# Emitting the output projection's weights earlier, with more raw buffers, in a hybrid encoder layer

## The chip, the core and the metric

The kernel runs on one core of a Trainium2 chip. The metric is the device time of one execution in microseconds, as the median of the runs. The core has a matrix engine (TensorE, PE in the profile, with its weight loads shown apart as PEld), a vector engine (VectorE, DVE), a scalar engine (ScalarE, ACT), GpSimd (POOL) and a sync engine (SP) that here only issues transfers. Each engine works through its own queue in order; semaphores tie the queues together. ACT and POOL issue some transfers too.

## The reference, cut to what matters

One encoder layer on 1024 tokens of width 1024: a half-step feed-forward, a mixer with two groups of heads side by side, and a second half-step feed-forward. The change sits in the mixer's output projection.

```
h = pre2(x); z = h @ w_in
y_att  = attention_group(z[..., :1536])          # 512 columns, normalised per head, times attn_out_g
y_rwkv = rwkv7_group(z[..., 1536:])              # 512 columns: two scans summed, group norm, bonus, gate
mix = concatenate([y_att, y_rwkv], -1) @ w_out   # w_out: 1024 x 1024
h = h + rmsnorm(mix, mix_post_g)
f = swiglu(rmsnorm(h, ffn2_pre_g), w_gate, w_up, w_down)
h = h + 0.5 * rmsnorm(f, ffn2_post_g)
```

All of it is float32 in and out. The first 512 rows of `w_out` meet the attention half, the last 512 the scan's half.

## The kernel before

**Products.** Float32 operands are split in two parts of a reduced form, `h` (a copy rounded by ACT) and `l` (the rest, by DVE), and a product is three matrix products: `h*h`, `h*l`, `l*h`. `load` (L181) issues the transfer and `split` (L184) does the two steps; so each weight tile costs one transfer into a raw buffer, one ACT and one DVE instruction. For the attention half the split also multiplies by a gain (L1054, L1055).

**Order on the queues.** The program is written against a framework that takes the source's order as a rank, works out by itself in which order each engine's instructions are issued, places the semaphores, and lets the tiles of a pool wait for what lay in the same memory before. A pool's tag has a fixed number of buffers; a tile waits until the one that held its buffer is read for the last time. Pools are stacks on two sides of the on-chip memory.

**The stages round the change**, in `run` (L1163):

- Values, attention and the scan's inputs are made; a step `prep(n)` (L783) prepares block `n` of eight, `solve(n)` (L850) inverts its triangular systems on DVE in some 62 short instructions, `merge(n)` (L875) assembles the inverses, and `chain(n)` (L918) carries the scan's state through the block. `upto(m)` (L1283) runs `prep` and `solve` up to block `m`. Lines L800 and L810 to L832 are parts of `prep`, L866 to L870 of `solve`, L937 to L970 of `chain`.
- `out_weights` (L1041) loads and splits eight tiles of 128 x 512 (four row groups `k`, two column halves `dh`) with tag `wor` for the raw tile (one buffer), `woh` and `wol` for the parts (eight each). For the attention half it is called at L1294, behind `upto(2)`.
- `project_attended` (L1066) takes one tile of 128 tokens of the attention's result through its half of the projection: two groups of twelve matrix products into `po` (L1064), copied to `yao` (L1083; the same tag `wor`, so the same single buffer) and stored to `hp`. It runs once per block, two at the first, between the chains.
- `finish_half` (L1035) runs four units of the group norm (`finish_unit`, L975): six loads of 256 KB and one of 128 KB (`f_y`, `f_k`, `f_r`, `f_v`, `f_sg`), two sums on POOL (L994, L997), five small products on PE (L995 to L1025), and at the end the split (L1028) into the operand `x`. The pool `fin0` holds three units at a time. Units 0 and 1 fill the columns of row tiles 0 and 1, units 2 and 3 those of 2 and 3, and so on. The first half is called at L1310, the second at L1322; units of the second half need the last block's chain.
- `out_weights` for the scan's half is called between them, at L1320, with a pool `wo` of its own.
- `out_project` (L1086) takes the eight row tiles: load of the row from `hp` (L1090), 24 matrix products `pw` (L1064), sums on DVE (L1095), and then `done(i)`: `post` (L251 to L258: load of `res`, a sum of squares on ACT into `junk`, L256, L257, store), `pre` of the row before (L266), and the turning for the next feed-forward (L330). From the fifth row tile on, POOL forms sums and differences of rows (L339 to L343).

**Where the pools lie.** Bytes per partition in the program before:

```
left    scan 75,392-108,544   (its last tile, xs: 106,496-108,544)
        eo  108,544-150,016   (rs, wor/yao 1 x 2,048, woh, wol, yat, yah, yal)
   then rows2 75,264-108,032, wo 108,032-142,848 (wor 1 x 2,048, woh, wol),
        hand2 142,848-159,488 (b_mix_post_g, res, junk, rs1, b_ffn2_pre_g)
right   fin0 152,512-194,560 (g2w, three each of f_y0, f_y1, f_k0, f_k1, f_r, f_v, f_sg), closed before hand2 opens
```

Of the kernel before, what the change touches and what calls it, by code (L numbers as in the profile page):

```python
# [10 lines left out]
F32 = mybir.dt.float32  # L11
# [152 lines left out]
class _Kernel:  # L164
# [202 lines left out]
    def down(self, p, ring, rows, psum, hid, wd, ws, order, done):  # L367
# [11 lines left out]
        def right(n, m):  # L379
            if n > 3:  # L380
                src = ws[n - 4, m]
            else:
                r, c = {1: (0, 0), 2: (1, 0), 3: (1, 1)}[n]
                src = wd[(2 * m + r) * 128:(2 * m + r + 1) * 128, c * 512:(c + 1) * 512]
            return [q.rearrange("p a b -> p (a b)") for q in self.halves(
                p, self.slab(ring, src.rearrange("p (a b) -> p a b", a=4)), ("gh", "gl"), GB)]

        def left(n, m, cols):
            raw, h, l = (ring.tile([128, 512], dt, name="g" + t, tag=t, bufs=b)[:, :cols.stop - cols.start]
                         for t, dt, b in (("raw", F32, RAW), ("wh", F32R, WB), ("wl", F32R, WB)))  # L390
            self.load(raw, hid[n - 1, m, :, cols])
            self.split(h, l, raw)
            return h, l
# [9 lines left out]
        for q, n in enumerate((1, 2, 6, 5, 3, 7, 4)):  # L403
            W = {}
            for g in [(0, 1), (2, 3)] if n == 4 else [(0, 1, 2, 3)]:
                ps = [psum.tile([128, 512], F32, name="pd", tag=("d", "gu")[q % 2]) for i in g]
                for m in range(NM):
                    h, l = left(n, m, slice(g[0] * 128, g[-1] * 128 + 128))
                    if m not in W:
                        W[m] = right(n, m)  # L410
                    wh, wl = W[m]
                    for x in range(len(g)):
# [42 lines left out]
    def project_attention(self, p, psum, x, streams):  # L455
# [10 lines left out]
        zts = [p.tile([128, 4, 128], F32, name="zts", tag="zts", bufs=6) for t in range(6)]  # L466
        W = {0: q_w, 1: list(zip(kh, tiles(1, "l")))}
        for b in (1, 0):
            hl = self.columns(p, b * 512, 512, W[b], bufs=11)
            if b:  # L470
# [567 lines left out]
            for g in range(2):  # L1038
                self.finish_unit(p, psum, b, g, x, g2w)

    def out_weights(self, p, k0, gain=None):  # L1041

        nc, W = self.nc, []
        for k in range(4):
            hl = []
            for dh in range(2):
                raw = p.tile([128, 512], F32, name="wor", tag="wor", bufs=1)
                self.load(raw, self.io["w_out"][0][(k0 + k) * 128:(k0 + k + 1) * 128, dh * 512:(dh + 1) * 512])
                h = p.tile([128, 512], F32R, name="woh", tag="woh", bufs=8)
                l = p.tile([128, 512], F32R, name="wol", tag="wol", bufs=8)  # L1050
                if gain is None:
                    self.split(h, l, raw)
                else:
                    nc.scalar.activation(h, raw, AF.Copy, scale=gain[:, k:k + 1])  # L1054
                    nc.vector.scalar_tensor_tensor(l, raw, gain[:, k:k + 1], h, op0=OP.mult, op1=OP.subtract)  # L1055
                hl.append((h, l))
            W.append(hl)
        return W
# [7 lines left out]
    def project_attended(self, p, c, psum, t, W, rs_a):  # L1066

        nc, V, A, T = self.nc, self.nc.vector, self.nc.scalar, self.nc.tensor
        rows = slice(t * 128, (t + 1) * 128)
        y = p.tile([128, H, 64], F32, name="yat", tag="yat")  # L1070
        self.load(y.rearrange("p a b -> p (a b)"), self.ya_d[rows, :])
        V.tensor_tensor(y, y, rs_a[:, t * H:(t + 1) * H][:, :, None].to_broadcast([128, H, 64]), op=OP.mult)
        q = psum.tile([128, 4, 128], F32, name="yq", tag="eo")
        for k in range(4):
            T.transpose(q[:, k, :], y.rearrange("p a b -> p (a b)")[:, k * 128:(k + 1) * 128], self.ident)
        h, l = (p.tile([128, 4, 128], F32R, name="ya" + c, tag="ya" + c) for c in "hl")
        A.activation(h, q, AF.Copy)
        V.tensor_tensor(l, q, h, op=OP.subtract)
        for dh in range(2):
            ps = psum.tile([128, 512], F32, name="po", tag="eo")  # L1080
            self.out_products(ps, W, dh, h, l, slice(0, 128))
            o = p.tile([128, 512], F32, name="yao", tag="wor", bufs=1)
            A.copy(o, ps)  # L1083
            self.nc.scalar.dma_start(self.hp_d[rows, dh * 512:(dh + 1) * 512], o)

# [77 lines left out]
    def run(self):  # L1163
# [5 lines left out]
        with self.top as top:  # L1169
# [5 lines left out]
            x = self.operand(xp, xp)  # L1175
            x0 = self.io["x"][0]

            with ExitStack() as st:
# [11 lines left out]
                with self.tc.high_priority():  # L1190
                    gain = self.spread_row(hand, ring, pt, "ffn1_pre_g")
# [26 lines left out]
                p = self.pool(st, "ffn1")  # L1218
# [17 lines left out]
                x = x2  # L1236
# [40 lines left out]
            eo = self.pool(s_eo, "eo")  # L1277
# [5 lines left out]
            def upto(m):  # L1283
                while nxt[0] <= min(m, NB - 1):
                    n = nxt[0]
                    blk[n] = self.prep(n, sp, pp, R0 if n in (3, 5) else B0)
                    self.solve(n, sp)
                    nxt[0] += 1

            upto(1)  # L1290
            rs_a = self.rstd(eo, self.ss_a.rearrange("p a b -> p (a b)"), NT * H, 1.0 / HD, EPS)
            self.merge(0, blk[0], sc, pm)
            upto(2)
            WA = self.out_weights(eo, 0, self.aog)  # L1294
            for n in range(NB):
                if n:
                    self.merge(n, blk[n], sc, pm)
# [2 lines left out]
                for t in ([0, 1] if n == 0 else [n + 1] if n + 1 < NT else []):  # L1300
                    self.project_attended(eo, sc, pe, t, WA, rs_a)
            s_sr.close()
# [4 lines left out]
            x = self.operand(xr, xr, n=4)  # L1307
            fi = self.pool(s_fi, "fin0", 3, **R)
            pf = self.pool(s_pa, "ps_f", 3, space=PSUM, **R)
            self.finish_half(fi, pf, 0, x)  # L1310
            s_pe.close()
            s_eo.close()
            s_sc.close()
# [1 line left out]
            st = ExitStack()  # L1315
# [1 line left out]
            rows = self.pool(s_xn, "rows2", 8)  # L1317
            hr = self.row_tiles(rows)
            h2 = {t: hr[i] for i, t in enumerate(self.order)}
            W = self.out_weights(self.pool(st, "wo"), 4)  # L1320
            psum = self.pool(st, "ps_3", 2, space=PSUM)
            self.finish_half(fi, pf, 1, x)  # L1322
            s_fi.close()
            s_pa.close()
# [6 lines left out]
            for j in range(2):  # L1331
                for n in (1, 2):
                    gate_up.ready[n, j] = self.halves(wf, self.slab(wf, gate_up.source(j, 0, n - 1), bufs=2, queue=nc.gpsimd),
                                                      bufs=4)
# [37 lines left out]
            with ExitStack() as st:  # L1372
# [12 lines left out]
                p, hand = self.pool(st, "ffn2"), self.pool(st, "hand3")  # L1385
# [49 lines left out]
```

## Time and profile before

| | us |
|---|---|
| median of 3 runs | 2390.91 |
| lowest and highest run | 2389.86, 2396.3 |
| profiled execution, its own time | 2398.21 |
| span of its trace | 2396.4 |

A row of the timeline has the start, the duration, the engine, the line, the operation, what is written and read, how many like it were merged, and in brackets how long the engine had been idle before and what ended the wait. In the view of one tile, each group of instructions has its count, shortest, median and longest duration in ns, and first and last start. SPq, ACTq and POOLq are the queues' own work, transfers issued above all. A line can be that of a helper that many parts call: L182 is every load on SP, L186 and L187 every split, L1064 every product of the output projection. So the tile's name says which part is meant: `po` is the attention half's sum, `pw` the scan half's.

### The profile page before, as it was taken

Reading aid. Unit: us, or ns where it says so; the run is one execution under the profiler, and the core shown is the slowest. Engines: PE = TensorE matmul, PEld = TensorE weight load, DVE = VectorE, ACT = ScalarE, POOL = GpSimd, SP = SyncE. Lnnn points to the kernel's source line nnn. Section 1 sums busy time; section 2 is a strip of 40 time slices with the busy share of each in tenths; the row PEclk is TensorE's granted clock in tenths of the full one; section 3 lists DMA queues with packets and bytes.
Section 4 is the critical chain, followed back from the end, with each engine's and each line's share of the span. In section 5 each row is a group of like instructions: output and inputs, shape, how many; then the busy total and the mean of one; then the engine's idle time right before and its main releaser. Section 6 shows DMA issues by size and latency. Waiting matters only on the chain. (4 is left out here: it accounts for less than half of the span.)

```text
span 2396.4 us, 39330 instructions
## 1 busy us (share of the span) xinstructions
PE 2233.1 (93%) x14532; PEld 1801.5 (75%) x14532; DVE 1778.9 (74%) x2917; ACT 1030.6 (43%) x1918; POOL 572.8 (24%) x668
## 2 busy tenths in 40 slices
PE   6999999999999998999986788898989999999997
PEld 4788888788786676778775577775768888887886
DVE  8899999865675345666556766746889999997565
ACT  4422333354676304556544444445442233335452
POOL 6244344500000010111101121132234443442000
PEclk8999999999999998999995698789989999999999
DMA  5344544576743415322366766558534544448655
GB/s 155 110 172 150 171 158 156 181 257 194 227 152 133 161 50 157 84 71 72 91 173 174 177 157 166 146 173 268 186 107 172 180 150 167 164 152 268 194 189 180
DMA packets 359763, 386.03 MB, mean 161 GB/s; under 512 B 73618, under 2 KB 268050, under 8 KB 359572
## 3 DMA queue, kind: packets, MB, share of 16 engines
q1 hardware_dynamic: 311968, 284.82, 39.5%
q0 software_dynamic: 27248, 86.05, 9.7%
q10 hardware_dynamic: 20356, 12.66, 1.8%
q8 instruction: 114, 1.87, 0.3%
q14 instruction: 77, 0.63, 0.1%
HBM read 257.53 MB, written 125.89 MB: 160 GB/s over the span
## 5 line engine op out<-in xcount | busy, mean ns | idle before, releaser
L186 ACT ACTIVATE wh<-raw 128x512 fp32r<-128x512 f32 (+1 forms) x273 | 168.2, 627 | 261.8 <-DVE raw L62 94.0
L81 PE MATMUL gu<-xh,wh 128*128 128x512 f32 x704 | 277.2, 394 | 2.3 <-ACT wh L186 1.1
L187 DVE TENSOR_TENSOR wl<-raw,wh 128x512 fp32r<-128x512 f32 (+1 forms) x273 | 275.6, 1013 | 2.1 <-ACT wh L186 1.2
L81 PE MATMUL gu<-xh,wl 128*128 128x512 f32 x704 | 275.9, 392 | 0.0
L81 PE MATMUL gu<-xl,wh 128*128 128x512 f32 x704 | 275.7, 392 | 0.0
L415 PE MATMUL pd<-gl,gwh 128*128 128x512 f32 x616 | 240.5, 390 | 2.5 <-DVE gl L187 2.5
L415 PE MATMUL pd<-gh,gwh 128*128 128x512 f32 x616 | 239.6, 390 | 0.6 <-DVE row L86 0.6
L415 PE MATMUL pd<-gh,gwl 128*128 128x512 f32 x616 | 239.8, 389 | 0.0
L86 DVE TENSOR_TENSOR row<-gu,row 128x512 f32<-128x512 f32 x308 | 206.3, 682 | 26.1 <-PE gu L81 24.2
L187 DVE TENSOR_TENSOR gwl<-graw,gwh 128x512 fp32r<-128x512 f32 (+1 forms) x176 | 117.9, 672 | 128.4 <-ACT gwh L186 125.7
L116 POOL DMA_DIRECT2D d_hid<-row x154 | 84.7, 551 | 473.3 <-DVE row L114 446.2
L186 ACT ACTIVATE gwh<-graw 128x512 fp32r<-128x512 f32 (+1 forms) x176 | 101.4, 576 | 188.4 <-PE pd L415 157.5
L81 PEld LDWEIGHTS gu<-xh,wh 128*128 128x128 f32 x704 | 133.5, 190 | 31.6 <-ACT xh L186 2.0
L81 PEld LDWEIGHTS gu<-xl,wh 128*128 128x128 f32 x704 | 133.4, 189 | 27.5
L81 PEld LDWEIGHTS gu<-xh,wl 128*128 128x128 f32 x704 | 133.1, 189 | 27.6
L415 PEld LDWEIGHTS pd<-gl,gwh 128*128 128x128 f32 x616 | 115.6, 188 | 28.0 <-DVE gl L187 4.3
L415 PEld LDWEIGHTS pd<-gh,gwh 128*128 128x128 f32 x616 | 115.6, 188 | 25.3 <-DVE row L86 1.0
L415 PEld LDWEIGHTS pd<-gh,gwl 128*128 128x128 f32 x616 | 115.7, 188 | 23.8
L187 DVE TENSOR_TENSOR gl<-raw,gh 128x512 fp32r<-128x512 f32 x160 | 112.3, 713 | 17.0 <-ACT gh L186 16.7
L94 ACT ACTIVATE row<-row 128x512 f32<-128x512 f32 x44 | 27.8, 633 | 221.3 <-DVE row L86 217.5
L145 POOL TENSOR_TENSOR ws<-ws 128x512 f32<-128x512 f32 x88 | 114.2, 1298 | 1.1
L186 ACT ACTIVATE gh<-raw 128x512 fp32r<-128x512 f32 x160 | 98.0, 621 | 33.7 <-DMA raw<-in_ffn_w_down_dram 21.8
(354 smaller groups left out, 5345.7 us busy)
## 6 DMA issues: line engine op xcount, KB each, us to landing
d_hid<-row POOLq DMA_DIRECT2D x154, 256.0 KB, 2.4
graw<-d_hid SPq DMA_DIRECT2D x132, 256.0 KB, 3.0
raw<-in_ffn_w_gate_dram SPq DMA_DIRECT2D x88, 256.0 KB, 3.0
raw<-in_ffn_w_up_dram SPq DMA_DIRECT2D x88, 256.0 KB, 3.3
ws<-in_ffn_w_down_dram SPq DMA_DIRECT2D x88, 256.0 KB, 4.5
d_ws<-ws POOLq DMA_DIRECT2D x88, 256.0 KB, 2.3
raw<-d_ws SPq DMA_DIRECT2D x88, 256.0 KB, 2.7
raw<-in_ffn_w_down_dram SPq DMA_DIRECT2D x66, 256.0 KB, 3.6
```

Source lines behind the costliest of these rows:

```text
L81: self.K.nc.tensor.matmul(ps, a[:, k, :], b[:, k, :], start=(k == 0 and i == 0), stop=(k == 3 and i == 2))
L86: add = lambda o, x: V.tensor_tensor(o, ps, x, op=OP.add)
L94: A.activation(y[:, 0], y[:, 0], AF.Silu)
L116: put = lambda n, y: G.dma_start(self.hid[n - 1, j // 2], y)
L145: G.tensor_tensor(o, a, b, op=OP.subtract)
L186: self.nc.scalar.activation(h, src, AF.Copy)
L187: (eng or self.nc.vector).tensor_tensor(l, src, h, op=OP.subtract)
L415: T.matmul(ps[x], a[:, ts], b, start=(m == 0 and k == 0), stop=(m == NM - 1 and k == 2))
```

## The change

`out_weights` takes the number of raw buffers as an argument: two for the attention half (and for `yao`, which shares the tag), four for the scan's half. The call for the attention half moves ahead of `upto(1)`, so ahead of the second block's `prep` and `solve`. The first `finish_half` moves behind the scan half's `out_weights`, so that these weights stand ahead of all eight units; with that it also moves behind the closing of the scan's pools and the opening of `rows2`, `wo` and `ps_3`. No instruction is added or left out. `eo` grows by 2,048 bytes per partition and `wo` by 6,144.

```diff
-    def out_weights(self, p, k0, gain=None):
+    def out_weights(self, p, k0, bufs, gain=None):
...
-                raw = p.tile([128, 512], F32, name="wor", tag="wor", bufs=1)
+                raw = p.tile([128, 512], F32, name="wor", tag="wor", bufs=bufs)
...
-            o = p.tile([128, 512], F32, name="yao", tag="wor", bufs=1)
+            o = p.tile([128, 512], F32, name="yao", tag="wor", bufs=2)
...
+            WA = self.out_weights(eo, 0, 2, self.aog)
             upto(1)
             rs_a = self.rstd(eo, self.ss_a.rearrange("p a b -> p (a b)"), NT * H, 1.0 / HD, EPS)
             self.merge(0, blk[0], sc, pm)
             upto(2)
-            WA = self.out_weights(eo, 0, self.aog)
             for n in range(NB):
...
             pf = self.pool(s_pa, "ps_f", 3, space=PSUM, **R)
-            self.finish_half(fi, pf, 0, x)
             s_pe.close()
             s_eo.close()
             s_sc.close()
...
-            W = self.out_weights(self.pool(st, "wo"), 4)
+            W = self.out_weights(self.pool(st, "wo"), 4, 4)
             psum = self.pool(st, "ps_3", 2, space=PSUM)
+            self.finish_half(fi, pf, 0, x)
             self.finish_half(fi, pf, 1, x)
```

## The prediction

> **What bounds the kernel now.** I read the page first, then busy time by stage, then the timeline of each engine round the two places that the change touches, and the chain that ended last for the end.
>
> ```profile
> span 2396.4 us, 39330 instructions
> PE 2233.1 (93%) x14532; PEld 1801.5 (75%) x14532; DVE 1778.9 (74%) x2917; ACT 1030.6 (43%) x1918; POOL 572.8 (24%) x668
> ```
>
> TensorE is busy 93% overall, but the edit stands where it is not full. By stage (columns: PE, PEld, DVE, ACT, POOL busy, granted clock, DMA share, GB/s):
>
> ```profile
> 1260.00:1303.00 43.00, 26.15 (x308) 22.78 (x308) 23.37 (x56) 21.98 (x38) 10.29 (x16) 0.52 0.65 165
> 1303.00:1352.00 49.00, 34.47 (x425) 29.60 (x425) 39.55 (x130) 18.15 (x35) 0.00 (x0) 0.71 0.69 178
> 1596.00:1624.00 28.00, 24.28 (x482) 19.38 (x481) 6.66 (x14) 14.23 (x26) 8.87 (x7) 0.88 0.90 286
> 1652.00:1680.00 28.00, 22.42 (x89) 13.49 (x87) 19.84 (x32) 14.34 (x28) 5.78 (x5) 0.94 0.88 290
> 1680.00:1723.00 43.00, 41.08 (x198) 33.62 (x197) 39.14 (x58) 24.39 (x51) 3.86 (x4) 1.00 0.53 183
> ```
>
> At 1260 to 1352 the scan of blocks starts: latency first (no engine over 61%), then VectorE at 81%. From 1596 to 1680 the last block and the eight units of the group norm run, with the DMA engines at 0.88 to 0.90. From 1680 to 1723 the output projection runs with PE at 96% and DVE at 91%.
>
> **Edit 1, the attention half's weights ahead of the second block.** Eight loads of 256 KB, eight ACT splits, eight DVE splits move; none is added.
>
> ```profile
> 1262.36 6.70 SPq L615 DMA_DIRECT2D d_vt<-vts  x8
> 1269.10 0.53 SPq L182 DMA_DIRECT2D wor<-in_w_out_dram  x1
> 1270.44 0.78 SPq L182 DMA_DIRECT2D in<-d_rk  x1
> 1279.47 0.69 DVE L810 TENSOR_TENSOR pr<-in,e 128x512 f32<-128x512 f32 x1 [6.11 <-DMA in<-d_rk]
> ...
> L1055 DVE SCALAR_TENSOR_TENSOR wol<-wor,c_attn_out_g,woh 128x512 fp32r<-128x512 f32 x4 | 3.0, 745 | 0.0
> ...
> 1354.84 0.79 PE L1064 MATMUL po<-woh,yah 128*128 128x512 f32 x1 [13.87 <-ACT woh L1054]
> 1358.70 0.72 ACT L1054 ACTIVATE woh<-wor,c_attn_out_g 128x512 fp32r<-128x512 f32 x1 [1.08 <-DMA wor<-in_w_out_dram]
> 1357.95 0.69 DVE L822 TENSOR_TENSOR bk<-th_a,th_w 128x512 f32<-128x512 f32 x1
> 1358.78 4.27 PE L830 MATMUL lp<-pr,bk 64*128 64x128 f32 x29 [1.51 <-DVE bk L822]
> ```
>
> The first weight load already leaves at 1269.10, ahead of loads that stand before it in the source; the last split runs at 1358.70. One raw buffer hands the eight tiles through in 90 us. With two buffers and a higher place they would be through some 40 us earlier. The tempting price is the 13.87 us that PE sat before `po`. I count it at nothing: the next PE work of the scan, `lp` at 1358.78, waited in its turn for `bk` of L822, which VectorE finished at 1358.64 after a stretch in which it was the full engine. Without the `po` wait PE would wait there for DVE. If that cover is false, up to 13.9 us are to be had (a rival below).
>
> What VectorE itself gets back in its full stretch, 1303 to 1352, is four splits of 745 ns, 3.0 us. What it may cost is in the stage before: the load of `in` at 1270.44 reached DVE 9.0 us later, through engines busy 0.65 of the time, and the second block waited for it. Two of the eight weight loads fell before 1303; now most do. Their landing time bounds what one more in front of `in` can cost:
>
> ```profile
> DMA to landing us min/median/max: 2.6/3.1/8.1
> ```
>
> So edit 1 lies between -3.0 and +3.1 us. I take -1: four splits off a full engine are surer than a load falling just before `in`, since SP was itself held by the stores of L615 until 1269. The second `yao` buffer (copies at L1083) takes waits off ACT, which is busy 18.15 of 49 us; ACT's own slack covers them, so nothing.
>
> **Edit 2, the other half's weights ahead of the units, four raw buffers.**
>
> ```profile
> 1613.96 1.27 POOL L994 TENSOR_TENSOR f_y<-f_y,f_y 128x512 f32<-128x512 f32 x1 [2.51 <-DMA f_y<-d_y]
> 1619.13 1.04 PE L952 MATMUL xu<-xs,tt 64*64 64x64 f32 x30
> 1627.43 0.47 SPq L182 DMA_DIRECT2D wor<-in_w_out_dram  x1
> 1630.27 1.02 PE L995 MATMUL yc<-f_y,k_cen 128*128 128x512 f32 x2
> 1643.70 0.73 PE L1064 MATMUL pw<-wol,xh 128*128 128x512 f32 x1 [3.05 <-DVE wol L187]
> 1657.29 0.82 SPq L182 DMA_DIRECT2D row<-d_hp  x2
> 1661.61 0.43 SPq L182 DMA_DIRECT2D f_y<-d_y  x1
> 1675.84 0.33 SPq L182 DMA_DIRECT2D wor<-in_w_out_dram  x1
> 1677.38 0.50 PE L1064 MATMUL pw<-woh,xh 128*128 128x512 f32 x1 [0.78 <-DVE row L1095]
> L187 DVE TENSOR_TENSOR xl<-f_y,xh x8: 675/682/1126, 1626.1 to 1679.7; 128x512 fp32r<-128x512 f32 x8
> ```
>
> Now the loads drip from 1627 to 1676, between those of the units, and each `pw` group is stopped by the next tile. The eight units end their split at 1626.1 to 1679.7, so (1679.7 - 1626.1)/7 = 7.7 us apart. The first two row tiles need only units 0 and 1, the first four only units 0 to 3; by that step their columns are ready at about 1634 and 1649, yet the first group had to wait for the tile loaded next to last and its L1095 released PE at 1677.4. With the weights in place by about 1632 (the last block's reads of `xs`, which lies under the first raw buffer, end at 1620 with L952, and eight tiles with four buffers are two rounds of loads), those products can go into PE's gaps: 28 - 22.4 = 5.6 us of them in 1652 to 1680, and as much before. A row tile costs 5.46 us of `pw`. So two, perhaps three, row tiles are done by 1680 instead of one, as far as the rows of `hp` (not issued until 1657) allow.
>
> But what follows the products (L256, L257, L266) cannot start earlier than the units end. The pool of this stage, `hand2`, lies on top of `wo`; with three more raw buffers it moves up 6,144 bytes, and `res`, `junk` and the gain then lie on `f_y0` and `g2w` of the units. So the first `res` load, which went at 1676.7, now waits for the last unit's split.
>
> ```profile
> 1679.74 0.69 DVE L187 TENSOR_TENSOR xl<-f_y,xh 128x512 fp32r<-128x512 f32 x1 [0.76 <-ACT xh L186]
> DMA to landing us min/median/max: 4.0/4.3/6.7
> 1693.40 0.15 DVE rs L246
> 1688.97 1.22 DVE L257 TENSOR_TENSOR row<-row,res 128x1024 f32<-128x1024 f32 x1
> 1703.10 5.46 PE pw L1064 x24
> 1708.56 0.87 PE pt L330 x8
> L256 DVE SCALAR_TENSOR_TENSOR row<-row,rs,b_mix_post_g x8: 1276/1278/2060, 1687.1 to 1727.5; 128x1024 f32<-128x1024 f32 x8
> L257 DVE TENSOR_TENSOR row<-row,res x8: 1204/1220/2305, 1689.0 to 1736.8; 128x1024 f32<-128x1024 f32 x8
> L266 DVE SCALAR_TENSOR_TENSOR row<-row,rs,b_ffn_pre_g x8: 1277/1280/1760, 1694.7 to 1743.0; 128x1024 f32<-128x1024 f32 x8
> 1719.11 1.28 DVE L266 SCALAR_TENSOR_TENSOR row<-row,rs,b_ffn_pre_g 128x1024 f32<-128x1024 f32 x1
> 1720.54 1.28 POOL L339 TENSOR_TENSOR row<-row 128x512 f32<-128x512 f32 x1 [32.35 <-DVE row L266]
> ```
>
> Start: split ends 1680.4, `res` lands 4.3 us later, so the first L257 at about 1684.8 instead of 1688.97: -4.2 us. Step: the chain shows a row tile every 5.46 + 0.87 = 6.33 us, PE's own time. With the first products done, DVE sets it: 1.28 + 1.22 + 1.28, two splits of 0.69 and two small ones of 0.15 are 5.5 us, and the single `res` buffer allows one per 1.22 + 4.3 = 5.5 us; I take 5.6. Four steps lie between the first tile and the fifth, whose L266 at 1719.11 lets POOL begin its sums: 4 x (6.33 - 5.6) = -2.9 us. From there to the next stage POOL sets the pace (the fifth tile released it after 32.35 us of waiting), and that tail moves as a whole. So -7.1 us. Bounds: 0, if the row tiles come no sooner, and -15, if three of the four are out of PE's way (3 x 6.33 = 19.0, less the 4.2 that `hand2` holds back).
>
> What it may cost lies in 1596 to 1624, where the weights pass the units' loads on SP. Eight loads are 2.10 MB; at the 286 GB/s of that row 7.3 us. Nearly all of it is covered: POOL had the third unit's data at 1613.96, but PE, busy with the last block, made its first product at 1630.27; and the same bytes no longer run at 1627 to 1676. On ACT the eight splits move into a stage where it is busy 14.23 of 28 us. I take 0, with +7.3 as the bound.
>
> The Trainium skill's page "DMA: Bandwidth & Descriptors" (section "Issuing engines are not separate DMA queues") speaks against this edit: transfers of all issuers end on the same 16 engines and interleave, so nothing is gained in transfer time by putting a load first. The trace agrees: 0.90 busy in that stage. By that page's 358 GB/s per core (section "Specifications") the same 2.10 MB would be an estimate of 5.9 us.
>
> **Sum.** -1 - 7 + 0 = -8 us. Against the profiled execution (span 2396.4, its own time 2398.21 with 1.8 us round the span) that is 2390.2; against the median of the runs, 2390.91, it is **2383 us**. The profiled one is 7 us over the median, so the difference is what I carry over, not the sum.
>
> **Rivals.**
>
> *Nothing arrives (within 3 us, 2391).* The order on the queues is made at compile time and the source's order is only a rank in it: the first load at 1269.10 shows it. If the rows of `hp`, still last on SP, keep L1095 and with it the two PSUM banks of `pw` until 1665, or if the units yield to the products on PE and end later by what the row tiles gain, the stage ends as now. For: DMA at 0.88 to the very end of the units. Against: PE's 5.6 us of gaps.
>
> *Slower: the units' loads are late (+7, 2398).* One place: SP and the DMA engines at 1596 to 1624. SP works in order; a weight load whose memory is under the last block's `xs` or `yao` stands there until these are free, and every `f_` load behind it stands too; ACT, in order as well, then waits in a split for a tile while the last block's copies queue behind it. The units end at 1687, and all after that is late by the 7.3 us, since `hand2` starts with their end; the step of 5.6 gives nothing back when `pw` of the second half comes late as well. It decides as soon as the last unit's loads, issued at 1661.61, slip by more than the 7 us gained. For: 0.90 busy. Against: the first units were waiting for PE, not for data.
>
> *More than forecast (-20, 2371).* The `po` wait of 13.87 us was real, or half 0 is wholly done by 1680: either adds about 12 us. Against the first stands `bk`; against the second, `hand2`.
>
> **How the numbers follow.** Forecast 0.46, nothing arrives 0.20, slower 0.19, more 0.15. A measurement of this kernel tells about 0.3%, 7.2 us, from no change, so faster begins at 2383.7. Of the forecast's 0.46 two thirds lie beyond that (0.31) and one third short of it (0.15); with the rivals: faster 0.31 + 0.15 = 0.46, same 0.15 + 0.20 = 0.35, slower 0.19. The forecast's own range is 2377 to 2388. The range that is to hold the time 8 times in 10 reaches to the slower case's 2398 and to 2371; it takes in both bounds of edit 1 (6 us apart) and the 0 and -15 of edit 2.
>
> **What would show it.** Right: weight loads of the first half through before about 1310 and no `po` wait over 5 us; the second half's `wol` done before 1640; two or more row tiles' L1095 before the last unit's `xl`; the first L257 within 6 us of that `xl`; and POOL's first sum 5 to 9 us earlier against that of before. Wrong: the last `xl` later than 1683 with everything ahead equal; L1095 still first after the units; or a span up to the last block that moves by more than 3 us, which would say that edit 1 was mispriced.

## The result, and the profile after

| runs of one comparison | us, median (lowest to highest) | ratio to before, 95% interval |
|---|---|---|
| before, 12 runs | 2391.69 (2384.81 to 2397.57) | |
| changed kernel, 12 runs | 2390.36 (2383.02 to 2394.92) | 0.9990 [0.9976, 1.0005] |
| before, 29 runs, a later comparison | 2394.21 (2386.46 to 2407.86) | |
| changed kernel again, 12 runs | 2391.67 (2385.31 to 2398.82) | 0.9982 [0.9967, 0.9998] |

By the two intervals the change is worth between 8 us less and 1 us more, likeliest 2 to 4 us less. The forecast of 2383 us is not what happened; 2391, the time of the rival "nothing arrives", is. The stated range, 2371 to 2398, holds the time, but it held no change at all as well, so this speaks for none of the steps that led to 2383. The profiled execution of the changed kernel took 2390.49 us.

Its page, the first line and the busy time of the engines:

```profile
span 2388.6 us, 39318 instructions
PE 2232.5 (93%) x14532; PEld 1803.1 (75%) x14532; DVE 1781.5 (75%) x2917; ACT 1030.7 (43%) x1918; POOL 570.3 (24%) x668
```

The engines' work is the same as before within 3 us. Busy time by stage in the changed kernel, for the two stretches of edit 1, with the columns of the prediction:

```profile
1260.00:1303.00 43.00, 23.06 (x272) 19.78 (x270) 27.43 (x63) 22.82 (x37) 10.28 (x16) 0.56 0.81 205
1303.00:1352.00 49.00, 40.01 (x488) 34.07 (x486) 39.23 (x115) 25.30 (x50) 0.00 (x0) 0.79 0.73 183
```

The DMA share of the first stretch went from 0.65 to 0.81: the weights now load there. In the second PE does 40.01 us where it did 34.47, since `po` no longer stands still. From 1596 on the same clock times do not compare, since this trace is some 9 us ahead there.

**The place of edit 1.** Timeline rows of the kernel before (first `pr` of the second block, its first `bk`, the first block's `d_y`), which the prediction did not show:

```profile
1268.12 0.69 DVE L810 TENSOR_TENSOR pr<-in,e 128x512 f32<-128x512 f32 x1
1290.07 0.69 DVE L822 TENSOR_TENSOR bk<-th_a,th_w 128x512 f32<-128x512 f32 x1
1332.07 0.93 ACTq L972 DMA_DIRECT2D d_y<-yb  x2
```

and of the changed kernel, with the group of the first half's eight `wol` splits last:

```profile
1271.93 0.68 DVE L810 TENSOR_TENSOR pr<-in,e 128x512 f32<-128x512 f32 x1
1273.13 1.76 SPq L182 DMA_DIRECT2D wor<-in_w_out_dram  x2
1274.99 0.54 SPq L182 DMA_DIRECT2D in<-d_rk  x1
1284.74 0.68 DVE L810 TENSOR_TENSOR pr<-in,e 128x512 f32<-128x512 f32 x1
1295.44 0.69 DVE L822 TENSOR_TENSOR bk<-th_a,th_w 128x512 f32<-128x512 f32 x1
1334.95 0.93 ACTq L972 DMA_DIRECT2D d_y<-yb  x2
1355.56 3.75 PE L830 MATMUL lp<-pr,bk 64*128 64x128 f32 x24 [5.84 <-DVE Ti L868]
...
L1055 DVE SCALAR_TENSOR_TENSOR wol<-wor,c_attn_out_g,woh x8: 744/751/752, 1278.0 to 1300.8; 128x512 fp32r<-128x512 f32 x8
```

The whole traces are 3.8 us apart by here, so count from the first `pr`. The next `pr` follows after 12.8 us instead of 11.4 (before, 1279.47 in the prediction), the `bk` after 23.5 instead of 22.0: two `wor` now stand ahead of `in` on SP. The first `d_y` leaves 63.0 us after it against 64.0. The eight splits are over at 1301.6 instead of 1360. The 13.87 us in front of `po` are gone, and PE waits 3.26 us for `yao` and 5.84 us for the solve on VectorE (`Ti`) instead, so about 9 of those 13.87 us went into other waits.

The other traces of the experiments below show more than this pair. In the eight with edit 1 the first `d_y` comes 62.4 to 64.4 us after the first `pr`, in the four with the old place 58.0 to 64.0. The second `d_y` comes 124.2 to 129.5 us after it in the eight, and 128.5 to 134.6 in the four. So the first block gains nothing, and the stretch behind it, in which the `po` wait lay, gains some 4 us (medians of 125.1 and 128.9).

**The place of edit 2.** Loads on SP and the second and third unit's splits:

```profile
1619.04 2.55 SPq L182 DMA_DIRECT2D wor<-in_w_out_dram  x4
1627.21 0.38 SPq L182 DMA_DIRECT2D f_y<-d_y  x1
...
1626.49 0.69 DVE L187 TENSOR_TENSOR xl<-f_y,xh 128x512 fp32r<-128x512 f32 x1
1637.99 0.68 DVE L187 TENSOR_TENSOR xl<-f_y,xh 128x512 fp32r<-128x512 f32 x1
```

The weights go out between the units' loads, four at once, and the third unit comes 11.5 us after the second (before 9.7). The next one follows it after 4.4 us, so the eight units end as they did, 55.0 us after the last block's `d_y` (before 55.7). Then the output projection: the second half's `wol` group, the last unit's `xl`, and what follows it.

```profile
L187 DVE TENSOR_TENSOR wol<-wor,woh x8: 684/691/1064, 1625.2 to 1634.1; 128x512 fp32r<-128x512 f32 x8
1670.48 0.69 DVE L187 TENSOR_TENSOR xl<-f_y,xh 128x512 fp32r<-128x512 f32 x1 [0.16 <-ACT xh L186]
1675.61 0.75 POOL L284 DMA_DIRECT2D raw<-in_ffn_w_gate_dram  x1 [16.10 <-DVE wl L187]
1677.02 1.22 DVE L257 TENSOR_TENSOR row<-row,res 128x1024 f32<-128x1024 f32 x1
1680.78 0.80 PE L1064 MATMUL pw<-woh,xh 128*128 128x512 f32 x1 [3.53 <-DVE row L1095]
1683.07 1.28 DVE L266 SCALAR_TENSOR_TENSOR row<-row,rs,b_ffn_pre_g 128x1024 f32<-128x1024 f32 x1
1711.02 1.28 DVE L266 SCALAR_TENSOR_TENSOR row<-row,rs,b_ffn_pre_g 128x1024 f32<-128x1024 f32 x1 [0.52 <-DMA d_h<-row]
1712.41 2.40 DVE L256 SCALAR_TENSOR_TENSOR row<-row,rs,b_mix_post_g 128x1024 f32<-128x1024 f32 x1
1712.45 1.28 POOL L339 TENSOR_TENSOR row<-row 128x512 f32<-128x512 f32 x1 [34.31 <-DVE rs L246]
```

The first `L266` comes 12.6 us after the last `xl` (before 1694.65 - 1679.74 = 14.9). But the four steps to the fifth take 27.9 us (before 24.5), so POOL's sums begin 42.0 us after the `xl`, against 40.8. Two waits stand out. One is the preload of the next stage's gate weights: four slabs through two raw buffers, so the third is asked for only at 1675.61, when VectorE has split the first; ACT stands 3.67 us at its split, and `L1095`, behind `wl` in VectorE's order, releases PE after 3.53 us. In the kernel before PE had hardly any products ahead and stood 0.97 us at the same place. After the 3.53 us the granted clock was 0.50 (a window with the columns of the stage tables), and the twelve products of half a row took 5.3 us. The next twelve, from 1686.9 on, took 2.8 at a clock of 1.00:

```profile
1680.78:1686.07 5.29, 5.29 (x13) 4.02 (x14) 4.24 (x7) 1.96 (x4) 0.00 (x0) 0.50 0.52 204
```

The other wait is in the chain that ended last (start, duration, what):

```profile
1691.95 1.28 DVE row L256
1693.24 1.15 DVE row L257
1694.40 2.85 DMA d_h<-row
1697.35 1.28 DVE row L266
1698.74 1.28 DVE row L256
```

One row tile is a ring: `L257` writes `row`, the store of that row takes 2.85 us, and `L266` overwrites `row` in place, so it waits for the store; `L256` of the next tile stands behind it on VectorE. 1698.74 - 1691.95 = 6.8 us, more than PE's 6.33. In the kernel before there is no such ring: there VectorE's order has `L256` of the next tile ahead of `L266`, so the store passes beside other work.

```profile
1702.22 1.22 DVE L257 TENSOR_TENSOR row<-row,res 128x1024 f32<-128x1024 f32 x1
1704.02 1.28 DVE L256 SCALAR_TENSOR_TENSOR row<-row,rs,b_mix_post_g 128x1024 f32<-128x1024 f32 x1
1706.47 1.28 DVE L266 SCALAR_TENSOR_TENSOR row<-row,rs,b_ffn_pre_g 128x1024 f32<-128x1024 f32 x1
```

Which order a kernel gets, the framework decides; the ring's order is in the traces of the changed kernel, of edit 2 alone and of edit 1 with four slab buffers.

### The profile page after: what moved, and what is told of

It is laid out like the page before. It is cut to its first block, busy times and chain, and to the rows that moved or that the text cites. A ratio compares the mean times of both kernels' runs of the same rounds, so it can differ in the third digit from the quotient of the medians.

```text
span 2388.6 us, 39318 instructions
## 1 busy us (share of the span) xinstructions
PE 2232.5 (93%) x14532; PEld 1803.1 (75%) x14532; DVE 1781.5 (75%) x2917; ACT 1030.7 (43%) x1918; POOL 570.3 (24%) x668
## 5 line engine op out<-in xcount | busy, mean ns | idle before, releaser
L86 DVE TENSOR_TENSOR row<-gu,row 128x512 f32<-128x512 f32 x308 | 206.6, 683 | 23.9 <-PE gu L81 23.2
L94 ACT ACTIVATE row<-row 128x512 f32<-128x512 f32 x44 | 27.9, 633 | 222.6 <-DVE row L86 218.9
```

The lines of the kernel that those rows point to most:

```text
L86: add = lambda o, x: V.tensor_tensor(o, ps, x, op=OP.add)
L94: A.activation(y[:, 0], y[:, 0], AF.Silu)
```

## The experiments

All were run against the kernel before in the same comparison; its medians there were 2393.44 (35 runs, the first four experiments), 2394.03 (34 runs, the next four) and 2394.21 (29 runs, the rest). First each half of the change by itself.

**Edit 1 alone.** `out_weights(eo, 0, 2, self.aog)` ahead of `upto(1)`; the second half's call with one buffer, behind the first four units, as before.

> Edit 1 alone (attention half's weights ahead of the second block, two raw buffers; the scan half's weights as before). Theory A, the step after the products eats the gain of edit 2, so what is left of the change is edit 1: 2389 to 2391 (ratio 0.999 to 1.000), with all wol of the first half split within 30 us of the first load and the row step of the last stage 6.3 us as before. Rival B, edit 1 costs what edit 2 brings: 2395 to 2399 (1.002 to 1.003). Rival C, edit 1 brings most of it, as the one pair of traces has it between first solve and last chain (12 us less): 2380 to 2384 (0.995 to 0.997).

2388.70 us, ratio 0.9984 [0.9969, 0.9999]: -3.8 us, just beyond the good end of Theory A.

**Edit 2 alone.**

```diff
-            WA = self.out_weights(eo, 0, self.aog)
+            WA = self.out_weights(eo, 0, 1, self.aog)
...
-            self.finish_half(fi, pf, 0, x)
...
-            W = self.out_weights(self.pool(st, "wo"), 4)
+            W = self.out_weights(self.pool(st, "wo"), 4, 4)
+            self.finish_half(fi, pf, 0, x)
```

> Edit 2 alone (scan half's weights ahead of the units, four raw buffers). Theory A: 2390 to 2393 (0.9995 to 1.0005); the products of several row tiles are done before the last unit, but L257 then repeats every 6.8 to 6.9 us instead of 6.3, so POOL's first sum comes 39 to 41 us after the last unit's split, as before. Rival B: 2383 to 2386 (0.997 to 0.998), with L257 every 6.3 us or less. Rival C (edit 2 costs): 2396 to 2400.

2396.71 us, ratio 1.0019 [1.0004, 1.0033]: edit 2 costs 4.5 us, rival C. Its trace has the changed kernel's tail: first `L266` 12.5 us after the last `xl`, four steps in 28.0 us, POOL's sums over 32.2 us. Its units took 58.2 us from the last block's `d_y` (before 55.7), and from the last `xl` to the end of the trace it took 718.5 us (before 716.7): 2.5 and 1.8 us, together about the 4.5, by one trace each.

**The ring cut, in the changed kernel and in the one before.** The row's sum goes to the `res` tile (three of them), which is stored; `L266` then reads `res` and writes `row`, and waits for no store.

```diff
-        nc.vector.tensor_tensor(ft, ft, r, op=OP.add)
-        self.nc.sync.dma_start(store[rows, :], ft)
+        self.nc.vector.tensor_tensor(r, ft, r, op=OP.add)
+        self.nc.sync.dma_start(store[rows, :], r)
+        return r
```

> The changed kernel, with the sum of L257 written to the res tile (three buffers) instead of in place, so that L266 need not wait until the store of the row has read it. Theory A (the ring store 2.85, L266 1.28, L256 1.28, L257 1.15 and the small steps, 6.85 us, sets the step): the step falls to 5.5 to 5.9 us, POOL's first sum comes 4 to 6 us sooner after the last unit's split, and the time is 2384 to 2387 (0.997 to 0.998). Rival: the step is set by the order on VectorE or by PE whatever the store does: step 6.3 to 6.9, 2389 to 2392 (0.999 to 1.000).

> The kernel before with the same edit as in the run of the changed kernel with the sum apart. Theory A (before, PE's own 5.46 and 0.87 us set the step of 6.33): step 6.2 to 6.4, time 2390 to 2392 (0.9995 to 1.0005). Rival (the ring through the store set the step before as well): step 5.5 to 5.9, time 2386 to 2389 (0.998 to 0.999).

2391.72 us, 0.9995 [0.9981, 1.0009], and 2392.89 us, 1.0005 [0.9991, 1.0019]. The kernel before behaves as its Theory A has it: four steps in 25.4 us. The changed kernel did not gain the 4 to 7 us expected of it, and its time is that of the rival. The ring alone does not hold the stage. Its trace shows what took over (PE, the first product after the gate slabs; L1109 is L1095 with the lines shifted):

```profile
1688.19 0.79 PE L1078 MATMUL pw<-woh,xh 128*128 128x512 f32 x1 [5.17 <-DVE row L1109]
```

PE now stood 5.17 us at the slabs, where it had stood 3.53, and again the granted clock was 0.50 over the 5.3 us behind it.

**The slabs.** The preload of the gate weights gets four raw buffers instead of two (`bufs=4` in its call of `slab`): in the changed kernel; in the changed kernel with the ring cut as well (with two `res` tiles instead of three, for the memory); and in edit 1 alone.

> The changed kernel, and the four gate slabs that the feed-forward preloads in front of the output projection get four raw buffers instead of two. Theory S (in every kernel so far ACT and DVE stand in their order at the split of the third slab, which was asked for only when the first split had freed a buffer, and L1095 with PE's pw stands behind it; that is why the tail from the last unit's xl to POOL's first sum was 40 to 42 us in all of them): the wait goes, the first L257 to the fifth L266 shortens, tail 38 to 39.5 us, time 2387 to 2389 where the changed kernel stood at 2391. Rival R (the ring of one row, sum, store, L266, L256, is what sets the step of the changed kernel): tail 41 to 42 us, time 2390 to 2393. Rival N (VectorE is simply full after the last unit): the same, with DVE's idle time in that stage no smaller than before.

> Both waits out of the changed kernel: four raw buffers for the gate slabs, and L257's sum written to the res tile (two of them) so that L266 needs no store behind it. Theory S: as with four slabs alone, tail 38 to 39.5 us, 2387 to 2389, since the ring is hidden. Rival R: only the two together show it: tail 34 to 37 us, 2383 to 2387. Rival N: tail 40 to 42 us, 2390 to 2393.

> Edit 1 alone (attention half's weights early, two raw buffers; the other half's as before), and four raw buffers for the gate slabs. Theory S: the slab wait goes here too, tail 38 to 39.5 us, time 2385 to 2387 where edit 1 alone stood at 2388.7; edit 2 then costs 1 to 3 us beside it (the late third unit). Rival: without edit 2 the tile loaded last holds the products as long as the slabs do, so tail 40 to 41 us, time 2388 to 2390, and edit 2 pays once the slab wait is gone (the changed kernel with four slabs is then 2 to 4 us faster than this one).

2393.29 us, 0.9994 [0.9979, 1.0008]; **2385.22 us, 0.9961 [0.9947, 0.9975]**; 2393.91 us, 1.0010 [0.9996, 1.0025]. Theory S falls: the slabs alone bring nothing (tail 41.3 us, four steps still 27.5). For the two together Rival R's time holds, with a tail of 37.3 us. In edit 1 alone four slab buffers even cost some 6 us (1.0010 against 0.9984, from different comparisons), and the tail of 43.2 us fits neither line: its trace has the ring's order, with a step of 6.6 to 6.8 us.

These edits are not clean cuts. With four slab buffers in the changed kernel VectorE has no ring (`L256` stands ahead of `L266` there), and PE still stands 4.07 us at `L1095`, with a clock of 0.50 over the 5.2 us behind it. Rows of the kernel with both: slabs, last `xl`, first and fifth `L272` (that was L266), POOL's first sum, and the window behind PE's wait, which is still 3.21 us, but with the clock at 1.00.

```profile
1667.96 3.05 POOL L298 DMA_DIRECT2D raw<-in_ffn_w_gate_dram  x4 [6.54 <-issue]
1672.90 0.69 DVE L187 TENSOR_TENSOR xl<-f_y,xh 128x512 fp32r<-128x512 f32 x1 [0.16 <-ACT xh L186]
1684.49 1.28 DVE L272 SCALAR_TENSOR_TENSOR row<-res,rs,b_ffn_pre_g 128x1024 f32<-128x1024 f32 x1
1708.76 1.28 DVE L272 SCALAR_TENSOR_TENSOR row<-res,rs,b_ffn_pre_g 128x1024 f32<-128x1024 f32 x1
1710.19 1.28 POOL L353 TENSOR_TENSOR row<-row 128x512 f32<-128x512 f32 x1 [39.17 <-DVE row L272]
1682.84:1688.00 5.16, 4.05 (x21) 3.18 (x22) 5.16 (x8) 3.84 (x8) 0.00 (x0) 1.00 0.45 167
```

**The same two cuts without edit 2**, so edit 1, ring cut, four slab buffers.

> Edit 1 alone, the row's sum apart (two res tiles) and four gate slabs: the kernel of 2385.2 us without edit 2. Theory P (edit 2 pays once both waits behind it are gone, because four row tiles are then really ahead of PE): this one stands 3 to 6 us above the kernel with edit 2, 2388 to 2391, tail from last xl to POOL's first sum 40 to 42 us. Rival Q (cutting the two waits is what gained, edit 2 has no part in it): 2383 to 2387, tail 36 to 38 us.

2390.19 us, 0.9985 [0.9970, 1.0001]: Theory P. Last `xl`, first and fifth `L272`, POOL's first sum:

```profile
1671.16 0.69 DVE L187 TENSOR_TENSOR xl<-f_y,xh 128x512 fp32r<-128x512 f32 x1 [0.76 <-ACT xh L186]
1686.16 1.28 DVE L272 SCALAR_TENSOR_TENSOR row<-res,rs,b_ffn_pre_g 128x1024 f32<-128x1024 f32 x1
1712.40 1.28 DVE L272 SCALAR_TENSOR_TENSOR row<-res,rs,b_ffn_pre_g 128x1024 f32<-128x1024 f32 x1
1713.83 1.28 POOL L353 TENSOR_TENSOR row<-row 128x512 f32<-128x512 f32 x1 [44.90 <-DVE row L272]
```

Read from such rows, in us after the last `xl`:

| kernel | first L266 | four steps | VectorE busy in them | POOL's first sum | ratio to before |
|---|---|---|---|---|---|
| before | 14.9 | 24.5 | 24.0 | 40.8 | 1 |
| before, ring cut | 14.8 | 25.4 | 24.7 | 41.6 | 1.0005 |
| edit 1 alone | 15.0 | 24.7 | 23.9 | 41.1 | 0.9984 |
| edit 2 alone | 12.5 | 28.0 | 25.2 | 42.0 | 1.0019 |
| changed | 12.6 | 27.9 | 25.2 | 42.0 | 0.9990, 0.9982 |
| changed, ring cut | 11.8 | 28.0 | 23.5 | 41.2 | 0.9995 |
| changed, four slab buffers | 12.4 | 27.5 | 24.3 | 41.3 | 0.9994 |
| edit 1, four slab buffers | 14.9 | 26.9 | 24.8 | 43.2 | 1.0010 |
| changed, ring cut and four slab buffers | 11.6 | 24.3 | 23.7 | 37.3 | 0.9961 |
| edit 1, ring cut and four slab buffers | 15.0 | 26.2 | 23.8 | 42.7 | 0.9985 |

Edit 2 starts the rows 2.4 to 3.4 us earlier in every pair. In the kernels as they stood, the steps give that back and more; with only the ring cut they give most of it back (41.6 against 41.2, though these two differ in edit 1 as well), and with only the slab buffers part of it (43.2 against 41.3). With both it keeps 42.7 - 37.3 = 5.4 us. The times say the same, 0.9961 against 0.9985, some 5.7 us, though the two come from different comparisons and their intervals overlap a little. VectorE's busy time shows the floor: 23.5 to 25.2 us for the four steps in every kernel, so nearly all of the 24.3 us of the fastest row are VectorE's own work, as Rival N had it for all of them.

**Edit 1 taken apart.** The early place with one raw buffer, twice, and two buffers at the old place.

> The kernel before with the attention half's weights in front of the second block, but one raw buffer for them and for yao. Theory A (the place is what gains: the splits leave VectorE's full stretch and po no longer stops PE): 2388 to 2391 as with edit 1 whole, the first half's wol through before 1335, scan 353 to 359 us. Rival B (the second buffer is what gains, since one buffer still drips the loads in between those of the block): 2392 to 2395 like before, wol through after 1340, scan 361 to 368 us. Rival C (one buffer at the higher place holds the queue in front of the block's loads): over 2396.

> The early place with one raw buffer again, the same kernel. In its first runs it stood at 0.997 of before while its profiled execution had a scan of 363.6 us as before, and its runs had a mean granted clock of 0.956 where before had 0.951. Theory C (those runs fell together on a favourable clock; the edit itself gives nothing): 2391 to 2394 at a clock of 0.950 to 0.952. Rival D (the edit itself brings the clock or the time): 2383 to 2388 again, clock 0.955 or more.

> The kernel before with two raw buffers for the attention half's weights and for yao, at their old place behind the second and third block's preparation. Theory A (edit 1 gains only with the place and the buffer together, as the early place with one buffer left the scan at 363.6 us): time 2392 to 2395 like before, scan 360 to 368 us, the first half's wol through after 1330. Rival B (the buffer alone gains, the weights reach PE in time once two are in flight): 2388 to 2391, scan 352 to 358 us, wol through before 1320.

One buffer at the early place: 2383.88 us, 0.9970 [0.9948, 0.9992], and again 2385.11 us (6 runs), 0.9958 [0.9942, 0.9974], so better than any theory had it, and Rival D of the second look: it is the kernel, not the draw. Two buffers at the old place: 2393.83 us, 0.9998 [0.9987, 1.0008], nothing, as Theory A said. Rows of the second run with one buffer, to be read against those above:

```profile
1269.68 0.68 DVE L810 TENSOR_TENSOR pr<-in,e 128x512 f32<-128x512 f32 x1
1270.87 0.52 SPq L182 DMA_DIRECT2D wor<-in_w_out_dram  x1
1272.70 0.61 SPq L182 DMA_DIRECT2D in<-d_rk  x1
1280.69 0.69 DVE L810 TENSOR_TENSOR pr<-in,e 128x512 f32<-128x512 f32 x1 [0.37 <-DMA in<-d_rk]
1287.75 0.69 DVE L822 TENSOR_TENSOR bk<-th_a,th_w 128x512 f32<-128x512 f32 x1
1324.81 0.93 ACTq L972 DMA_DIRECT2D d_y<-yb  x2
```

From the first `pr`: the next after 11.0 us, `bk` after 18.1, the first `d_y` after 55.1 us, where the changed kernel has 12.8, 23.5 and 63.0. (The first profile of this kernel has 11.4, 18.3 and 55.8.) One `wor` fewer stands ahead of `in`, the rest trickle in behind the block's own loads, and the first block's output is 8 us earlier than in any of the eight traces with two early buffers. So the second buffer, not the place, delays the first block. But by the second `d_y` nothing of the 8 us is left: 128.7 and 125.3 us after the first `pr` with one buffer, 124.2 to 129.5 with two. The ratios put one buffer some 3 to 6 us ahead of two (0.9970 and 0.9958 against 0.9984), with intervals that overlap; what gains them stays open.

**The changed kernel again.**

> The changed kernel again, beside the others. Theory: 2389 to 2392, ratio 0.998 to 0.9995 (gain of edit 1 of about 4 us less the cost of edit 2), tail 40 to 42 us, POOL's sums over 29 to 33 us. Rival (the first comparison was a high draw and edit 2's cost is not there): 2384 to 2387.

2391.67 us, as in the table at the top; tail 41.9 us, POOL's sums over 32.3 us. The theory's line holds.

## Why the prediction was wrong where it was

- *Edit 1, "-1, between -3.0 and +3.1".* The sign was right and the term too small: -3.8 us, outside its own bound of -3.0, with an interval from -7.4 to -0.2. The price, a second load in front of `in`, is about 1.5 us at the next `pr` and at `bk`, within the 3.1 us allowed for it. The gain was put at four splits of VectorE's full stretch, and the `po` wait at nothing. That it is wholly covered is not borne out: about 9 of its 13.87 us went into other waits, and the second `d_y`, which lies behind it, comes some 4 us sooner. How much of this is `po` and how much the splits the runs do not part. The sign "a span up to the last block that moves by more than 3 us" cannot be read: that `d_y` comes 8.5 us earlier in one profile of the changed kernel and 1.3 in the other.
- *Edit 2, start, "-4.2".* Right in sign, -2.7 in size: the first `L257` came 6.5 us after the last `xl` (before 9.2), not within 6. The reason given, a `res` load that waits for the last unit's split, is not what held it: that load left at 1667.69, 2.8 us before the split ran. VectorE took the first `L256` and the second slab's split first. The weights were in place (splits over at 1634.8, "before 1640"), and four `L1095`, not one, ran ahead of the last `xl`.
- *Edit 2, step, "with the first products done, DVE sets it ... I take 5.6".* **This is the step that failed.** First, the sum for VectorE left out the two `L1095` of each row, 0.69 us apiece. VectorE was busy 24.0 of the 24.5 us of the four steps before, so about 6.0 us a row was its floor, and of the -2.9 no more than about one was to be had. Second, the step rose instead, to 7.0 us, for two reasons that the sum has no term for. PE, now ahead of the units, ran into `L1095` behind the gate slabs, stood 3.53 us and then made twelve products at a clock of 0.50, which took some 2.5 us more than the next twelve; they lie in the chain of the first step, which took 7.5 us. And VectorE's order became the ring of 1.28 + 1.15 + 2.85 + 1.28 us and some gaps, 6.8 us, in the three steps behind it. So -2.9 became +3.5. Neither of the two single edits took the slow clock away (0.50 after 5.17 us and after 4.07), and the kernel with both did. That the clock is the reason is argued from these traces; no run changes it alone, and each edit changed VectorE's order too.
- *The tail "moves as a whole".* No: POOL's sums took 32.3 us from first to last in both profiles of the changed kernel and 32.2 in edit 2 alone, against 28.9 before. While they ran, `L256` at 1712.41 took 2.40 us instead of 1.28, and the sixth `L266` came 10.3 us after the fifth, where before it was 6.8. POOL's last sum so ends 4.5 us later after the `xl` than before, and the next stage gives some 3 of them back: from the last `xl` to the end of the trace the two profiles take 718.1 us, the kernel before 716.7, and the kernel with both edits 713.1. POOL's first sum did come 8.1 us earlier in the trace, as the prediction asked, but by luck: the last `xl` was 9.3 us earlier, from the scan.
- *"The units' loads are late", the rival of 2398.* In part: the third unit was 1.8 to 4.5 us late in all six traces with edit 2. In four of them the units still ended as before (55.0 to 55.8 us after the last block's `d_y`); in edit 2 alone they took 58.2 us, and with four slab buffers 60.5, by one trace each; without edit 2 they took 53.8 to 57.1.
- *Sum.* -1 - 7 became about -4 and, of edit 2 on top of it, between -0.5 and +1.4 (0.9982 and 0.9990 against 0.9984; by itself +4.5). The rival "nothing arrives" had the time, not the reason: it put it on the rows of `hp` or on units that end later, but the units ended on time and the sums of two row tiles (four `L1095`) were early. What it said of the PSUM banks came near: `L1095` did hold PE, behind the slabs.

The fastest kernels measured are the changed one with the ring cut and four slab buffers (0.9961) and the one with edit 1 and a single buffer (0.9958 and 0.9970). Both together were not run.

## What to carry to other kernels

Before a bound is replaced by the next one in a sum, add up the next engine's busy time from the trace over the same steps; a list of its instructions made by hand forgets some. Then walk one whole turn of the loop for every buffer it rewrites in place: a store that reads a tile is a wait for whoever overwrites it, and whether it binds hangs on the order of the instructions round it. What is preloaded for the next stage stands in the same in-order queues as the work at hand. Where an engine is freed to run ahead, ask where it will stop next. Loads moved early can stand in front of the loads that the next step needs; with a second buffer there are more of them.

## What the runs showed that was not expected

The time goes with the granted clock, and from one execution of a kernel to the next that varies in the scan. Windows of the scan as a whole, for the two profiles of the changed kernel and then the two with one early buffer (columns as above):

```profile
1260.00:1620.00 360.00, 300.71 (x4620) 246.53 (x4618) 241.25 (x696) 170.64 (x316) 72.56 (x108) 0.81 0.66 174
```

```profile
1260.00:1620.00 360.00, 301.02 (x4540) 246.73 (x4540) 237.26 (x685) 166.41 (x308) 71.26 (x107) 0.78 0.65 168
```

```profile
1260.00:1620.00 360.00, 299.37 (x4601) 245.56 (x4602) 235.37 (x683) 166.00 (x308) 72.39 (x108) 0.82 0.64 169
```

```profile
1260.00:1620.00 360.00, 295.80 (x4643) 242.25 (x4644) 244.43 (x699) 173.40 (x322) 75.59 (x110) 0.85 0.68 179
```

From the last `zr` product to the last `d_y` these four took 355.1, 364.1, 363.6 and 349.3 us: the same kernel differs by 9 and by 14 us, more than any edit here. The runs show it too: twelve of the kernel with one early buffer go from 2373.96 us at a mean clock of 0.959 to 2396.55 at 0.952, and over all runs 0.001 of that clock is worth about 1.4 us (a fit with one level for each kernel and comparison). That kernel's runs had a mean clock of 0.956, the others 0.949 to 0.952, so part of its gain is the clock itself; whether the clock rises because the scan's waits are shorter, or the reverse, was not settled. The Trainium skill's page "TensorE: Matmul & The Clock Gate" (Part 1) says that the clock depends on how busy PE has been recently; that fits, with 0.98 over the first 1250 us and 0.99 from 1740 on in the changed kernel, where PE is busy 96% and 99% of the time, and with the 0.50 behind PE's waits of 3.5 to 5.2 us in the output projection. How long a wait must be for that was not measured.

POOL slows VectorE: 2.40 us for `L256` while POOL adds rows, 1.28 without. "SBUF — State Buffer" of the Trainium skill (section "Who interferes with whom") has the rule: a VectorE instruction with two SBUF inputs contends with a GpSimd instruction that reads SBUF. The trace agrees, and in the kernel before the same rows are longer too (`L256` 1.66 and 2.06 us while POOL adds).
